# A streaming-encoder trunk on one Trainium2 core: pooled-channel forms tied to earlier products, and row-norm roots in two GpSimd operations

## The chip, the core and the metric

One core of one Trainium2 chip runs the whole kernel. The metric is the device time of one execution in microseconds. The engines are named as in the profile: PE (TensorE, matrix products), ACT (ScalarE), DVE (VectorE), POOL (GpSimd), SP (SyncE, which here issues DMAs). Each engine works through its own queue of instructions in order, and waits at its head for what an instruction needs.

## What is computed

A sequence of 2048 rows of 1024 channels goes through one layer with two branches and a feed-forward part:

```python
xn = rmsnorm(x, norm1_g[l])
z = xn @ w_in[l]
u_pool, zq, zf, zi, zo, zg = jnp.split(z, splits, axis=-1)
gates = jax.nn.sigmoid(zg + b_gate[l]).reshape(B, S, N_BRANCHES, D_MODEL)
ya = pool_mixer(u_pool, pool_w[l], pool_scale[l]) @ w_pa[l]
yb = hgrn2_mixer(zq, zf, zi, zo, lower_bounds[l], hgrn_norm_g[l]) @ w_pb[l]
merged = gates[:, :, 0] * ya + gates[:, :, 1] * yb
x = x + merged @ w_o[l]
x = x + conv_glu_ffn(rmsnorm(x, norm2_g[l]), w_up[l], conv_w[l], conv_b[l], w_down[l])
return rmsnorm(x, final_g)
```

`pool_mixer` takes trailing means over windows of 2, 4, 8 and 16 rows, less the row itself, through a small matrix per group of 128 channels: 512 pooled channels. `hgrn2_mixer` is a gated linear recurrence with four heads. The change touches how the operands of `... @ w_pa` are made ready, the roots inside `rmsnorm`, and the order of a few instructions in the last `rmsnorm`.

## The kernel before

**Halves and blocks.** The sequence is worked in two halves of 1024 rows (their tiles are named x0, mf0, gr0, pa0 ... and x2, mf2, gr2, pa2 ...; in the profile's short names the number is often left out). A half has two blocks of 512 rows, hf = 0 and 1. Each half runs first the mixer (input projection, recurrence, the two branch projections pa and pb, the output projection wo) and then the feed-forward part (up, dn). Activations lie with channels on the 128 partitions and 512 rows along the free axis, so almost every tile is 128 x 512.

**Products by seven.** A projection of two blocks by two groups of channels is one *unit*: a 2 x 2 product of blocks in Strassen's manner, seven products P1 to P7 in place of eight, in the order P1, P6, P5, P7, P2, P4, P3 (`ORDER`). Each product needs one *form* of the activations, a block or a sum or difference of blocks: P1 takes B11, P2 B21, P3 B22, P4 T4, P5 T1, P6 T2, P7 T3. A unit has three banks of PSUM: X for P1 and P2, Z for P6, P7 and P4, V for P5 and P3. Between products DVE reads a bank into a temporary: u2 after P6 (L1202), u3 after P7 (L1206). The next product on Z is written over what they have read: P7 waits for u2, P4 for u3.

**Precision.** Every operand is split in two fp32r parts, high and low, and a product takes three matmuls (high x high, high x low, low x high). `split` makes the parts of a form: the high part by a cast on ACT (L659), the low part by a subtraction on DVE (L660), and the subtraction needs the cast. Weights come by DMA into `raw` tiles, some are summed there by POOL (L446), and are split in the same way by L231 (ACT) and L232 (DVE) into `ops` tiles, six of which are alive.

**What runs around the change.** After the last unit of the input projection (a gate unit, gr0_7 in half 0) comes the pa projection of the pooled channels. It runs in two rounds d = 0, 1 of two units each, seven products per unit. A product of pa's first unit has k = 2 pieces, six matmuls, and the second unit's product follows it with the same form. The forms of pa, B11 to B22, two tiles each (j = 0, 1: names like mf0T40 and mf0T41, with h or l behind them for the part), are made by `pa_task`: it loads the eight tiles of pooled channels (`mx`) that were stored to DRAM earlier, takes differences (`minus`, L1479 on DVE, t3 on POOL) and splits them. Meanwhile the fourth head of the recurrence ends: its small matmuls (po, pv) stand between PE's large ones, its norm root on POOL (L693, L694), its gated output ot on DVE (L1141), and its transposes pt on PE.

**What sets the order.** The kernel is written as one main line of matmuls and a set of tasks, generators that are advanced by one step every six matmuls (`tick`). `yield n` puts a task's next step n ticks later. `place[0]` counts products from the last gate unit's P1 on: 1 to 7 there, then 8 for pa's P1, 9 P6, 10 P5, 11 P7, 12 P2, 13 P4, 14 P3. `pa_task` starts at the gate unit's P1 and waits before each form until `place[0]` has come to a number. A form's instructions get a dependency on the matmul last written (`in_turn`), which only the scheduler sees: the scheduler, which fills the engines' queues ahead of the run by its own timeline, doesn't put them ahead of it. `behind` is a dependency of the same kind between two named instructions. So the numbers in `pa_task` move instructions within the queues of ACT, DVE and POOL, and once the queues are fixed nothing overtakes.

**Row norms.** `row_rstd` (L697) takes 128 rows: two squares on ACT with their sums in two columns, then the root of mean square on POOL. `norm_rows` scales the rows by it (L719). The final norm of the last half is `final_last` (L1776): squares on ACT, root by `Sqrt` on ACT (L1785) and one refinement on DVE, then one half of the rows' channels scaled on ACT (`scale`, L1796), the other on DVE (L1804); `scale` of one tile of rows is written down during the next tile's `final_last`.

## Time and profile before

| | before |
|---|---|
| median of 3 runs | 2529.55 us (2528.21 to 2531.17) |
| profiled execution | 2528.86 us, its span 2527.1 us |
| mean granted clock of PE | 0.996 |
| PE busy | 2503.3 us, 99% of the span, 11460 instructions |
| PE weight loads | 2049.4 us, 81% |
| DVE busy | 1992.4 us, 79% |
| ACT busy | 1215.1 us, 48% |
| POOL busy | 814.2 us, 32% |

The span runs from the first to the last instruction of the profiled execution; its time has 1.8 us around that. Engines run beside each other, so the busy shares don't add up. In the views, a line such as `PE pa_Z L148 <- ACT mf0T41h L659` reads: a matmul into bank Z of pa (line 148 of the code) waited for the cast of form T4, second tile, high part (line 659) on ACT. A timeline row has its start, its length, engine, line, operation, output <- inputs and shape, and in brackets the idle time of that engine before it with what ended it. Rows of matmuls overlap, since they are pipelined; the step from start to start is what one costs.

### The profile page before, as it was taken

What the parts mean: (1) busy time and instruction counts of PE and PEld (TensorE: products, weight loads), DVE (VectorE), ACT (ScalarE), POOL (GpSimd) and SP (SyncE); (2) the same over time, 40 slices, a digit from 0 to 9 for tenths busy, and PEclk for the clock granted to TensorE, in tenths of its full rate; (3) what the DMA queues carried; (4) which work ended last, traced back from release to release, by engine and by line L of the source; (5) the groups of instructions that cost most, each with busy time, mean ns of one, the idle gap of its engine ahead of it and who ended that gap; (6) DMA issues with size and microseconds to landing.
All of it is one profiled execution on the core that took longest, in us unless ns stands there. A gap on an engine that the chain in (4) does not pass through costs nothing.

```text
span 2527.1 us, 35765 instructions
## 1 busy us (share of the span) xinstructions
PE 2503.3 (99%) x11460; PEld 2049.4 (81%) x11460; DVE 1992.4 (79%) x3528; ACT 1215.1 (48%) x2286; POOL 814.2 (32%) x1171
## 2 busy tenths in 40 slices
PE   9999999999999999999999999999999999999998
PEld 7888888788888888888888888887888888888886
DVE  7788878797998778875596778778979888778755
ACT  6534443434555544553554434543355555445534
POOL 4343453403354333541320202123033432325410
PEclk9999999999999999999999999999999999999999
DMA  8877787677898789897344343446343454447852
GB/s 272 272 199 225 209 222 232 203 226 244 204 257 238 228 225 243 270 358 237 113 155 153 106 133 109 144 157 229 125 157 119 151 153 135 151 133 245 321 166 97
DMA packets 252332, 493.76 MB, mean 195 GB/s; under 512 B 26544, under 2 KB 43056, under 8 KB 251824
## 3 DMA queue, kind: packets, MB, share of 16 engines
q1 hardware_dynamic: 184512, 313.60, 38.2%
q0 software_dynamic: 42656, 112.74, 17.4%
q10 hardware_dynamic: 24976, 65.13, 7.5%
q8 instruction: 91, 1.49, 0.2%
q14 instruction: 97, 0.79, 0.1%
HBM read 381.79 MB, written 187.17 MB: 225 GB/s over the span
## 4 chain that ended last, share of the span: by engine, by line
PE 97%; DVE 1%; ACT 1%; DMA 0%; issue 0%; POOL 0%; SPq 0%; DVEq 0%; POOLq 0%; ACTq 0%
PE dn_P L148 16%; PE up_Z L148 15%; PE up_V L148 10%; PE up_X L148 10%; PE wo_P L148 6%; PE gr_Z L148 5%; PE gr_V L148 4%; PE pb L148 4%; PE gr_X L148 4%; PE io_Z L148 3%; PE fr_Z L148 3%; PE io_V L148 2%; PE fr_V L148 2%; PE fr_X L148 2%; PE pl L1029 2%; PE pa_Z L148 1%
## 5 line engine op out<-in xcount | busy, mean ns | idle before, releaser
L231 ACT CAST ops<-raw 128x512 fp32r<-128x512 f32 x794 | 490.2, 620 | 867.4 <-PE dn_P L148 178.8
L232 DVE TENSOR_TENSOR ops<-raw,ops 128x512 fp32r<-128x512 f32 x794 | 588.1, 744 | 217.4 <-ACT ops L231 210.6
L1707 DVE SCALAR_TENSOR_TENSOR e<-h,cols,e 128x512 f32<-128x512 f32 x176 | 142.4, 813 | 30.4 <-ACT e L1705 23.9
L1705 ACT ACTIVATE e<-h,cols 128x512 f32<-128x512 f32 x176 | 142.2, 814 | 25.2 <-DVE h L1162 18.4
L1710 DVE SCALAR_TENSOR_TENSOR e<-h,cols,e 128x512 f32<-128x512 f32 x176 | 134.9, 776 | 2.5
L964 POOL DMA_DIRECT2D g_P<-dg_P x154 | 83.8, 545 | 161.7 <-PE dn_P L148 113.8
L1275 POOL TENSOR_TENSOR gf_P<-e,e 128x512 f32<-128x512 f32 x44 | 61.6, 1403 | 150.3 <-DVE e L1716 96.1
L446 POOL TENSOR_TENSOR raw<-raw,raw 128x512 f32<-128x512 f32 x36 | 51.1, 1420 | 154.7 <-DVE ops L232 138.7
L1275 POOL TENSOR_TENSOR gf_P<-gf_P,e 128x512 f32<-128x512 f32 x44 | 59.1, 1344 | 72.1 <-DVE e L1716 71.6
L1700 POOL COPY h<-h 128x2 f32<-128x2 f32 x88 | 40.0, 466 | 117.1 <-DVE h L1161 107.5
L1415 POOL TENSOR_TENSOR q<-q,qs 128x512 f32<-128x512 f32 x16 | 21.8, 1363 | 168.0 <-ACT qs L1414 165.6
L1714 ACT ACTIVATE e<-e 128x512 f32<-128x512 f32 x88 | 55.6, 632 | 37.1 <-DVE e L1710 37.0
L1702 POOL COPY hist<-h 128x2 f32<-128x2 f32 x88 | 35.1, 399 | 115.8 <-DVE h L1162 114.0
L1162 DVE TENSOR_TENSOR h<-up_u,up_V 128x512 f32<-128x512 f32 x88 | 60.1, 683 | 10.5 <-PE up_V L148 10.1
L1452 ACT ACTIVATE gt<-gt,cols 128x512 f32<-128x512 f32 x48 | 34.8, 725 | 66.8 <-DVE gt L1162 56.5
L1250 DVE TENSOR_TENSOR x<-x,wo_P 128x512 f32<-128x512 f32 x88 | 56.0, 682 | 12.0 <-PE wo_P L148 11.8
L1250 DVE TENSOR_TENSOR ac<-ac,dn_P 128x512 f32<-128x512 f32 x72 | 47.1, 682 | 17.5 <-PE dn_P L148 17.3
L1014 POOL COPY qm<-q 128x64 f32<-128x64 f32 x64 | 27.1, 446 | 99.6 <-DVE q L1046 19.6
L1700 POOL COPY h<-hist 128x2 f32<-128x2 f32 x88 | 45.2, 521 | 27.3 <-DVE m_T42l L660 27.2
L1200 ACT COPY up_e<-up_X 128x512 f32<-128x512 f32 x44 | 25.8, 586 | 57.7 <-PE up_X L148 50.5
L1730 POOL DMA_DIRECT2D dg_P<-gf_P x88 | 50.7, 576 | 8.1 <-POOL gf_P L1275 7.4
L1590 POOL TENSOR_TENSOR ya<-ya,gl 128x512 f32<-128x512 f32 x24 | 36.7, 1533 | 45.8 <-DVE ya L1587 20.8
(1372 smaller groups left out, 8130.6 us busy)
## 6 DMA issues: line engine op xcount, KB each, us to landing
g_P<-dg_P POOLq DMA_DIRECT2D x154, 256.0 KB, 6.0
raw<-in_w_up_t SPq DMA_DIRECT2D x132, 256.0 KB, 3.1
raw<-in_w_in_t SPq DMA_DIRECT2D x98, 256.0 KB, 3.2
dg_P<-gf_P POOLq DMA_DIRECT2D x88, 256.0 KB, 3.8
dg_P<-e SPq DMA_DIRECT2D x66, 256.0 KB, 3.6
raw<-in_w_dn SPq DMA_DIRECT2D x66, 256.0 KB, 4.1
x<-in_x SPq DMA_DIRECT2D x64, 256.0 KB, 5.2
gd<-gt ACTq DMA_DIRECT2D x64, 256.0 KB, 3.0
```

The costliest lines, as they stand in the source:

```text
L148: count[1] = pe.matmul(*args, **kw)
L231: self.mark = act.copy(hi, v)
L232: low = self.low = dve.tensor_tensor(lo, v, f32(hi), ALU.subtract)
L964: eng.dma_start(t, d)
L1162: return dve.tensor_tensor(dst, t, ps, ALU.add if how == "add" else ALU.subtract)
L1250: dve.tensor_tensor(t, t, ps[j], ALU.add if sg > 0 else ALU.subtract)
L1275: pin(eng.tensor_tensor(t, x0, x1, op))
L1700: pool.tensor_copy(h[:, 0:2], hist[:, mt] if hf == 0 else hs[s, 0][:, TB : TB + 2])
L1705: in_turn(act.activation(t, h[:, 2:], AF.Identity, bias=col(o_cb + mt), scale=col(o_cw + 4 * MF + mt)))
L1707: in_turn(second(dve.scalar_tensor_tensor(t, h[:, 1 : 1 + TB], col(o_cw + 2 * MF + mt), t, ALU.mult, ALU.add)))
L1710: dve.scalar_tensor_tensor(t, h[:, 0:TB], col(o_cw + mt), t, ALU.mult, ALU.add)
L1714: in_turn(act.activation(g, g, AF.Silu))
```

## The change

Three edits. In `pa_task` the numbers of `place[0]` go down: for B11 from 3 to 2, T2 4 to 3, T3's difference and T1 6 to 5, T3 8 to 6, B21 9 to 7, T4 10 to 8, B22 11 to 10, and the pauses of two ticks become one. In `row_rstd` the sum of the two squares and the constant is one POOL operation (a `tensor_scalar` with the first sum as its operand) where it was two, the first of them ahead of the second square. In `final_last` the scaling of the tile before is placed behind this tile's square root in the plan.

```diff
--- before.py
+++ after.py
@@ -699,10 +699,8 @@
         for hf in range(2):
             act.activation(junk[hf], halves[hf], AF.Square, scale=1.0 / 32.0,
                            accum_out=ss[:, hf : hf + 1])
-            if not hf:
-                pool.tensor_scalar(ss[:, 2:3], ss[:, 0:1], EPS, None, ALU.add)
         r = small.tile([P, 4], F32, tag="rstd", name=name + "r")
-        pool.tensor_tensor(r[:, 1:2], ss[:, 1:2], ss[:, 2:3], ALU.add)
+        pool.tensor_scalar(r[:, 1:2], ss[:, 1:2], ss[:, 0:1], EPS, ALU.add, ALU.add)
         last_root[0] = pool.tensor_tensor(r[:, :1], r[:, 1:2], neghalf[:, :1], ALU.pow)
         return r
 
@@ -1479,48 +1477,48 @@
                 in_turn(eng.tensor_tensor(x, x0, x1, ALU.subtract))
                 return x
 
-            while place[0] < 3:
+            while place[0] < 2:
                 yield 1
             for j in range(2):
                 form("B11", j, t[0, j])
                 yield 1
             t1, t2 = [], []
-            while place[0] < 4:
+            while place[0] < 3:
                 yield 1
             for j in range(2):
                 t1.append(minus("t1", j, t[1, j], t[0, j]))
                 t2.append(minus("t2", j, t[1, j + 2], t1[j]))
                 form("T2", j, t2[j])
-                yield 2
-            while place[0] < 6:
+                yield 1
+            while place[0] < 5:
                 yield 1
             t3 = [minus("t3", j, t[1, j], t[1, j + 2], pool) for j in range(2)]
             for j in range(2):
                 form("T1", j, t1[j])
                 yield 1
-            while place[0] < 8:
+            while place[0] < 6:
                 yield 1
             for j in range(2):
                 form("T3", j, t3[j])
-                yield 2
-            while place[0] < 9:
+                yield 1
+            while place[0] < 7:
                 yield 1
             for j in range(2):
                 form("B21", j, t[0, j + 2])
-                yield 2
-            while place[0] < 10:
+                yield 1
+            while place[0] < 8:
                 yield 1
             for j in range(2):
                 t4 = minus("t4", j, t[0, j + 2], t2[j])
                 form("T4", j, t4)
-                yield 2
-            while place[0] < 11:
+                yield 1
+            while place[0] < 10:
                 yield 1
             for j in range(2):
                 x = slot(f"mf{b0}_b22{j}")
                 in_turn(act.activation(x, t[1, j + 2], AF.Copy, scale=-1.0))
                 form("B22", j, x)
-                yield 2
+                yield 1
 
         emits = {"fq": emit_fq, "u": emit_u, "g": emit_g}
         oT = {}
@@ -1782,7 +1780,7 @@
             if not hf:
                 dve.tensor_scalar(ss[:, 2:3], ss[:, 0:1], EPS, None, ALU.add)
             r = small.tile([P, 4], F32, tag="rstd", name=f"f{b0}_{hf}_{j}r")
-            act.activation(r[:, 0:1], ss[:, 1:2], AF.Sqrt, bias=ss[:, 2:3])
+            root = act.activation(r[:, 0:1], ss[:, 1:2], AF.Sqrt, bias=ss[:, 2:3])
             dve.tensor_tensor(ss[:, 3:4], ss[:, 1:2], ss[:, 2:3], ALU.add)
             dve.reciprocal(r[:, 1:2], r[:, 0:1])
             dve.scalar_tensor_tensor(r[:, 2:3], r[:, 1:2], ss[:, 3:4], r[:, 1:2],
@@ -1792,12 +1790,14 @@
             rr = (b0 + hf) * TB + j * P
             o = [out[rr : rr + P, 512 * c : 512 * c + 512] for c in range(2)]
 
-            def scale():
-                act.activation(res[0], halves[0], AF.Copy, scale=r[:, 0:1])
+            def scale(other=None):
+                ins = act.activation(res[0], halves[0], AF.Copy, scale=r[:, 0:1])
+                if other is not None:
+                    behind(ins, other)
                 act.dma_start(o[0], res[0])
 
             while scales:
-                scales.pop()()
+                scales.pop()(root)
             if hf:
                 scales.append(scale)
             for c in range(hf, 2):
```

The order of instructions moves in the last part of the mixer, from the last gate unit's P5 to the wo projection, in both halves in the same way; elsewhere the roots lose one row each (32 rows of L703), and ACT's last rows change. Line numbers in the changed kernel are two lower from L705 to the middle of `final_last` (L1479 is L1477 there, L1206 is L1204).

DVE's queue around u3 of the last gate unit in half 0 (`ss`, `st` are the recurrence's state, `gt` a gate). Before:

```order
L660 TENSOR_TENSOR mf0B111l_4698<-mx0_1_4623,mf0B111h_4697 128x512
L1120 SCALAR_TENSOR_TENSOR st3_1_129<-ss0_3_4672,f0_3_3983,pv0_3_4667 128x128
L1206 TENSOR_TENSOR gr0_7_u3_4701<-gr0_7_Z_4609,gr0_7_e1_4607 128x512
L1162 TENSOR_TENSOR gt1_1_7_4703<-gr0_7_u3_4701,gr0_7_V_4645 128x512
L1479 TENSOR_TENSOR mf0_t10_4721<-mx1_0_4625,mx0_0_4621 128x512
L1479 TENSOR_TENSOR mf0_t20_4723<-mx1_2_4627,mf0_t10_4721 128x512
```

The same place now:

```order
L660 TENSOR_TENSOR mf0B111l_4674<-mx0_1_4615,mf0B111h_4673 128x512
L1477 TENSOR_TENSOR mf0_t10_4687<-mx1_0_4617,mx0_0_4613 128x512
L1118 SCALAR_TENSOR_TENSOR ss0_3_4668<-ss0_3_4668,f0_3_3975,pv0_3_4663 128x128
L1477 TENSOR_TENSOR mf0_t20_4689<-mx1_2_4619,mf0_t10_4687 128x512
L1118 SCALAR_TENSOR_TENSOR st3_1_129<-ss0_3_4668,f0_3_3975,pv0_3_4663 128x128
L660 TENSOR_TENSOR mf0T20l_4692<-mf0_t20_4689,mf0T20h_4691 128x512
L1477 TENSOR_TENSOR mf0_t11_4701<-mx1_1_4621,mx0_1_4615 128x512
L1477 TENSOR_TENSOR mf0_t21_4703<-mx1_3_4623,mf0_t11_4701 128x512
L660 TENSOR_TENSOR mf0T21l_4706<-mf0_t21_4703,mf0T21h_4705 128x512
L1204 TENSOR_TENSOR gr0_7_u3_4709<-gr0_7_Z_4601,gr0_7_e1_4599 128x512
L1160 TENSOR_TENSOR gt1_1_7_4711<-gr0_7_u3_4709,gr0_7_V_4637 128x512
```

The differences t10, t20, t11, t21 and both low parts of T2 now stand ahead of u3. On PE three rows of the fourth head (po1_3) now stand ahead of this unit's P4, and on POOL the differences t30, t31 ahead of the norm root ro0_3.

DVE's queue around the u2 of pa's second unit, first round, half 0. Before:

```order
L660 TENSOR_TENSOR mf0T31l_4898<-mf0_t31_4812,mf0T31h_4897 128x512
L1202 TENSOR_TENSOR pa0_0_u2_4901<-pa0_0_e1_4870,pa0_0_Z_4885 128x512
L1141 SCALAR_TENSOR_TENSOR ot1_3_4919<-po1_3_4829,ro1_3_4844,z1_3_4753 128x128 x4
L1202 TENSOR_TENSOR pa0_1_u2_4924<-pa0_1_e1_4879,pa0_1_Z_4903 128x512
L232 TENSOR_TENSOR ops134_4964<-raw97_4560,ops134_4964 128x512
L660 TENSOR_TENSOR mf0B210l_4944<-mx0_2_4633,mf0B210h_4943 128x512
L660 TENSOR_TENSOR mf0B211l_4968<-mx0_3_4635,mf0B211h_4967 128x512
```

The same place now:

```order
L660 TENSOR_TENSOR mf0B211l_4880<-mx0_3_4627,mf0B211h_4879 128x512
L1477 TENSOR_TENSOR mf0_t40_4901<-mx0_2_4625,mf0_t20_4689 128x512
L232 TENSOR_TENSOR ops134_4984<-raw97_4552,ops134_4984 128x512
L660 TENSOR_TENSOR mf0T40l_4904<-mf0_t40_4901,mf0T40h_4903 128x512
L1200 TENSOR_TENSOR pa0_0_u2_4907<-pa0_0_e1_4870,pa0_0_Z_4889 128x512
L1139 SCALAR_TENSOR_TENSOR ot1_3_4925<-po1_3_4829,ro1_3_4844,z1_3_4753 128x128 x4
L1477 TENSOR_TENSOR mf0_t41_4930<-mx0_3_4627,mf0_t21_4703 128x512
L660 TENSOR_TENSOR mf0T41l_4933<-mf0_t41_4930,mf0T41h_4932 128x512
L1200 TENSOR_TENSOR pa0_1_u2_4936<-pa0_1_e1_4883,pa0_1_Z_4909 128x512
L660 TENSOR_TENSOR mf0B220l_4958<-mf0_b220_4955,mf0B220h_4957 128x512
L660 TENSOR_TENSOR mf0B221l_4971<-mf0_b221_4968,mf0B221h_4970 128x512
```

The second unit's u2 now has both tiles of T4 and of B21 ahead of it, and the low parts of B22 stand right behind it. Before, T4's first difference came eight rows behind this u2.

ACT's queue in the last rows of the kernel, for the third tile of rows and the fourth (the number before the last in f2_1_2r and f2_1_3r counts them). Before:

```order
L1766 ACTIVATE fj2_1_3_1_24574,fss2_1_3_23933<-ac2_1_3_1_22752 128x512
L1796 ACTIVATE fo2_1_2_0_24548<-ac2_1_2_0_23350,f2_1_2r_24550 128x512
L1785 ACTIVATE f2_1_3r_24578<-fss2_1_3_23933 128x1
L1797 DMA out_0<-fo2_1_2_0_24548 128x512
L1796 ACTIVATE fo2_1_3_0_24576<-ac2_1_3_0_23352,f2_1_3r_24578 128x512
```

Now:

```order
L1764 ACTIVATE fj2_1_3_1_24542,fss2_1_3_23901<-ac2_1_3_1_22718 128x512
L1783 ACTIVATE f2_1_3r_24546<-fss2_1_3_23901 128x1
L1794 ACTIVATE fo2_1_2_0_24516<-ac2_1_2_0_23318,f2_1_2r_24518 128x512
L1797 DMA out_0<-fo2_1_2_0_24516 128x512
L1794 ACTIVATE fo2_1_3_0_24544<-ac2_1_3_0_23320,f2_1_3r_24546 128x512
```

The square root of the last tile now stands ahead of the scaling of the tile before it.

## The prediction

> **What bounds the kernel now.** I read the chain of waits first. It ends on TensorE:
>
> ```profile
> PE 97%; DVE 1%; ACT 1%; DMA 0%; issue 0%; POOL 0%; SPq 0%; DVEq 0%; POOLq 0%; ACTq 0%
> ```
>
> So only time in which PE stands, or runs at a lower clock, can be won. The waits of PE (summed us, count, longest) say where it stands:
>
> ```profile
> PE x_t L725 <- DVE x_xs L719: 2.5, 4, 1.0
> PE pa_Z L148 <- ACT mf0T41h L659: 1.7, 1, 1.7
> PE pa_Z L148 <- ACT mf2T41h L659: 1.7, 1, 1.7
> PE pa_Z L148 <- DVE mf0T41l L660: 1.3, 1, 1.3
> PE pa_V L148 <- ACT mf0B221h L659: 0.6, 1, 0.6
> ```
>
> Nearly all of them name forms T4 and B22 of the pooled channels, once in each half (mf0, mf2). The windows around them (us, PE busy, granted clock, DMA) give the price:
>
> ```profile
> 444.31:459.13 14.82, 14.82 (x71) 1.00 0.73 248
> 459.13:464.70 5.57, 1.90 (x5) 0.98 0.01 2
> 464.70:474.60 9.90, 8.19 (x18) 0.50 0.80 265
> 1712.49:1717.00 4.51, 1.41 (x5) 1.00 0.00 0
> 1717.00:1724.40 7.40, 5.68 (x12) 0.54 0.73 252
> ```
>
> PE stands for most of 5.57 us, and afterwards works for 9.9 us at half the clock; the second half shows the same with 7.4 us. PE's timeline (start, us) gives the ends of the stretch:
>
> ```profile
> 456.34 0.40 PE L148 MATMUL pa_X<-mf0B210h,ops 128*128 128x512 f32 x1
> 458.90 0.40 PE L148 MATMUL pa_X<-mf0B211h,ops 128*128 128x512 f32 x1
> 460.14 0.49 PE L148 MATMUL pa_Z<-mf0T40h,ops 128*128 128x512 f32 x1 [0.84 <-ACT mf0T40h L659]
> 461.51 0.40 PE L148 MATMUL pa_Z<-mf0T40h,ops 128*128 128x512 f32 x1
> 463.62 0.50 PE L148 MATMUL pa_Z<-mf0T41h,ops 128*128 128x512 f32 x1 [1.71 <-ACT mf0T41h L659]
> 466.40 0.63 PE L148 MATMUL pa_Z<-mf0T40h,ops 128*128 128x512 f32 x1
> 468.53 0.63 PE L148 MATMUL pa_Z<-mf0T41h,ops 128*128 128x512 f32 x1
> 475.36 0.40 PE L148 MATMUL pa_X<-mf0B110h,ops 128*128 128x512 f32 x1
> ```
>
> ```profile
> 1712.26 0.40 PE L148 MATMUL pa_X<-mf2B211h,ops 128*128 128x512 f32 x1
> 1727.61 0.40 PE L148 MATMUL pa_X<-mf2B110h,ops 128*128 128x512 f32 x1
> ```
>
> The twelve matmuls of P2 from 456.34 to 458.90 step by 2.56 / 11 = 0.232 us. The 24 of P4 and P3 behind them should take 5.6. In half 0 they run from 459.13 (458.90 + 0.23) to 475.36: 16.23, a loss of **10.6**. In half 1 from 1712.49 to 1727.61: 15.12, a loss of **9.5**. Together 20.1 us; no other stretch costs PE as much. The slow clock's part: from 466.40 to 468.53 five matmuls step by 0.426, so the 18 in half 0's slow window lost 18 × 0.194 = 3.5 and the 12 in half 1's 2.3; the rest is standing.
>
> The last forms are late because DVE and ACT reach them only when PE already wants them. Thresholds lower by one or two products cure that, if what is pushed aside has slack.
>
> **The change, part by part.**
>
> *Forms earlier: what is won.* T4's and B22's operations stand some ten DVE rows earlier. By the walk below the last T4 low ends at 458.1 and the last B22 low at 460.0, while PE comes to P4 at about 463 and to P3 at 465.7. Both waits and the slow clock behind them go: the whole 20.1 us. The loads are no bar. The pooled channels come by eight transfers:
>
> ```profile
> 420.71 4.93 SPq L964 DMA_DIRECT2D mx<-md  x8
> DMA to landing us min/median/max: 4.5/5.8/6.3
> ```
>
> The third, which the first difference needs at 431.7, is issued by 420.71 + 3/8 of 4.93 = 422.6 and there by 428.9; the last by 431.9, long before B21.
>
> *What is pushed aside.* DVE and POOL take turns where both read two operands from SBUF:
>
> ```profile
> 429.37 1.27 POOL L446 TENSOR_TENSOR w128s<-raw,raw 128x512 f32<-128x512 f32 x1
> 429.66 1.53 DVE L660 TENSOR_TENSOR mf0B110l<-mx,mf0B110h 128x512 fp32r<-128x512 f32 x1
> 431.37 0.68 DVE L660 TENSOR_TENSOR mf0B111l<-mx,mf0B111h 128x512 fp32r<-128x512 f32 x1
> 432.92 0.69 DVE L1206 TENSOR_TENSOR gr_u<-gr_Z,gr_e 128x512 f32<-128x512 f32 x1 [0.61 <-PE gr_Z L148]
> 436.97 0.48 PE L148 MATMUL gr_Z<-x_T40h,ops 128*128 128x512 f32 x1
> ```
>
> Alone, such a DVE operation is 0.68 long and the next starts 0.60 later (431.37 to 431.98 in the queue). The one at 429.66 ran beside POOL's sum and took 1.53: it ended 0.55 after POOL did. So I price 0.60 each, and a POOL sum in the way holds DVE until it ends, up to 1.27 us. The Trainium skill, page "SBUF — State Buffer", section "Who interferes with whom", says the same in its words: a DVE instruction with two SBUF inputs contends with a GpSimd one that reads SBUF, and the first one keeps the shared ports for its whole length. The rows above agree (1.53 against 0.68). That rule speaks against this change, which brings the forms' differences closer to POOL's sums.
>
> *Wait A, the last gate unit's P4.* It overwrites the bank that u3 (L1206) reads. u3 was at 432.92 after a free 0.61; now t20, T20l, t11, t21 and T21l and the first difference t10 stand ahead of it: six operations, 3.6 us. Without any hold u3 ends at 432.92 − 0.61 + 3.6 + 0.60 = 436.5. PE comes to P4 at 436.97 + 0.67 = 437.64, since three instructions of po1_3 (0.22 each, an estimate from the steps of the same multiplications around 436) now stand ahead: no wait. At most three POOL operations meet those six (the third sum and the two differences t3 that POOL now makes in front of its norm root): 3 × 1.27 = 3.8, so u3 ends at 440.3, a wait of 2.7. Walking the queues by their rows: B110l ends 428.65, B111l 430.45, POOL's third sum runs 430.45 to 431.7 and holds t10 to 432.3; POOL's t30 (432.25 to 433.5) holds t20 to 434.1; t31 (434.05 to 435.3) holds T20l to 435.9; then t11 436.5, t21 437.3, T21l 438.6 behind its ACT cast, u3 439.3. **A = 1.65 us**, bounds 0 and 2.7. I take the walk, near the upper end, because the collisions that it counts are of the kind seen at 429.66.
>
> *Wait B, the second pa unit's P7.* It overwrites the bank that its u2 reads:
>
> ```profile
> 451.38 0.68 DVE L1202 TENSOR_TENSOR pa_u<-pa_e,pa_Z 128x512 f32<-128x512 f32 x1
> 451.98 0.68 DVE L232 TENSOR_TENSOR ops<-raw,ops 128x512 fp32r<-128x512 f32 x1
> 454.88 0.48 PE L148 MATMUL pa_Z<-mf0T30h,ops 128*128 128x512 f32 x1
> ```
>
> u2 ended at 451.98; PE wanted the bank at 454.88, or now, 1.65 later, at about 456.6. Ahead of u2 now stand weight 134, B210l, B211l, t40, T40l, t41 and T41l as well: 7 × 0.60 = 4.2, so 456.2 without any hold and no wait. With A's delay in full (1.65 + 0.67) and one POOL sum (1.27) it is 459.8: 3.2. The walk: T31l and B210l, B211l end 451.25, t40 451.85, weight 134 453.0, T40l 453.6, the first unit's u2 454.3, ot1_3 455.25, t41 held by POOL's sum until 456.1 and done 456.7, its cast on ACT 457.45, T41l 458.1, u2 458.8. PE waits from 456.6: **B = 2.15 us**, bounds 0 and 3.2, and again I take the walk. Behind it 6 + 12 matmuls lead to P4 at 458.8 + 18 × 0.232 = 463.0, past T41l's 458.1.
>
> Does the clock fall at A or B? In half 0 PE stood through most of 459.13 to 461.51 (two matmuls in the 2.4 us, 1.9 of them idle), and the window to 464.70 still shows 0.98; it fell only after the further gap before 463.62 (2.11 from 461.51, less a step of 0.23: 1.88). Two lone waits of 1.65 and 2.15 with 17 us of work between them should not do it. The Trainium skill, page "TensorE: Matmul & The Clock Gate", section "What's actually happening", has the clock halved after an idle window of about 3.4 us. The trace fits that: the fall stands at the end of 459.13 to 464.70, where PE is busy 1.90 of 5.57. By it neither wait alone would halve the clock.
>
> *The roots of row norms* lose one of three POOL instructions in 32 places. PE waits for a norm only at the start (the row of x_t above), and there the last tile's scaling stands in DVE's queue behind a weight's low part, not behind the root:
>
> ```profile
> 10.58 0.52 POOL L703 TENSOR_SCALAR x_3ss<-x_3ss 128x1 f32<-128x1 f32 x1
> 11.18 0.28 POOL L705 TENSOR_TENSOR x_3r<-x_3ss 128x1 f32<-128x1 f32 x1
> 11.54 0.57 POOL L706 TENSOR_TENSOR x_3r<-x_3r,neghalf 128x1 f32<-128x1 f32 x1
> 11.71 0.69 DVE L232 TENSOR_TENSOR ops<-raw,ops 128x512 fp32r<-128x512 f32 x1 [0.30 <-ACT ops L231]
> 12.32 0.88 DVE L719 TENSOR_SCALAR x_xs<-x,x_3r 128x512 f32<-128x512 f32 x2
> ```
>
> L703 ran beside the row's second square and the root was done at 12.11, with DVE busy until 12.32: nothing to win. The new first operation is a tensor_scalar; if it takes L703's 0.52 where L705 took 0.28, the root comes at 12.35, 0.03 late. If the weight's part did not cover it, the same 0.24 would be lost. So 0, with bounds 0 and +0.24.
>
> *The tail.* The last square root waited on ACT behind the scaling of the tile before:
>
> ```profile
> 2520.20 0.19 ACT L1766 ACTIVATION_READ_ACCUMULATOR fj<-ac 128x1 f32 x1
> 2520.29 0.70 ACT L1796 ACTIVATE fo<-ac,f_2r 128x512 f32<-128x512 f32 x1
> 2520.90 0.28 ACT L1785 ACTIVATE f_3r<-fss 128x1 f32<-128x1 f32 x1
> 2522.05 0.75 DVE L1804 SCALAR_TENSOR_TENSOR fo<-ac,f_3r,fg 128x512 f32<-128x512 f32 x1
> ```
>
> It can start near 2520.35, right behind the sum of squares: **0.55 us** off a chain that nothing else covers. The scaling that it overtakes ends by 2521.3, ahead of the last one at 2522.05. Bounds 0.3 and 0.6.
>
> **The sum.** Per half A + B = 3.8 us in place of 10.6 and 9.5: 6.8 + 5.7 = 12.5. With the tail 13.05. The profiled execution took 2528.86 (span 2527.1, the rest lies around it), so 2515.8; it stands 0.7 under the median of the runs, 2529.55, which becomes **2516.5**.
>
> **The rivals.**
>
> *No wait at A and B* (the lower bounds): 20.1 + 0.55 = 20.65 less, 2508.9. For it: the collisions with POOL may fall otherwise, and t3 itself waits for free slots, which the walk gives it early. Against: the DVE rows alone use up nearly all the slack (436.5 against 437.64, and 456.2 against 456.6). Chance 0.13.
>
> *The clock falls at one of the new waits.* A fall costs what it cost now, 3.5 or 2.3. In one half or in both: 2516.5 + 2.3 to 2516.5 + 5.8, so 2518.8 to 2522.3. For it: 2.15 us is a longer single gap than the 1.88 that preceded the fall. Against: there it came on top of the two shorter gaps before 461.51. Chance 0.15.
>
> *The wait is only moved.* The slower end: u3 at A and u2 at B come at their upper bounds (2.7 + 3.2 = 5.9 per half) and each wait halves the clock for 9.9 us, now full of work (9.9 × 0.194 / 0.426 = 4.5 each): 14.9 per half, 29.8 against 20.1 + 0.55, so 9.1 us **slower**, 2538.7. It is one mechanism, DVE's queue of forms in front of the reads that free Z; it decides from a loss of 10.3 us per half on. For it: DVE's order here is fixed by the plan, u3 and u2 can't overtake. Against: it needs every POOL hold in full. Chance 0.05; what lies between (2524.5 to 2534.6, say A and B at their bounds with one fall in each half) has 0.07. That the places don't change the order can be left out: the order of DVE's queue does differ.
>
> **How the numbers follow.** The forecast with both waits near their walked sizes, 2513 to 2519, has 0.60. The range for 8 in 10 takes in the second case nearly whole and the first down to its bound: 2509 to 2523. 0.2% is about 5 us, what a measurement of this kernel can tell from no change: under 2524.5 is faster, 0.60 + 0.13 + 0.15 = 0.88; within it 0.07; slower 0.05.
>
> **What would show it.** Right: no wait of PE on T41 or B221, the clock at 1.00 from 444 to 480 and in the same place of the second half, one wait of 1 to 2.5 us before gr_Z's P4 and one before pa_Z's second P7, both released by DVE, and the tail's square root 0.6 earlier. Wrong: those two waits absent (then 2509), a granted clock near 0.5 right behind one of them (2519 and more), or PE waiting for a weight (ops) that DVE now splits later than the forms; that last would show that the DVE queue, not the forms, sets this stretch.

## The result, and the profile after

| | before | after |
|---|---|---|
| median | 2529.91 us (4 runs, 2528.21 to 2531.17) | 2513.73 us (4 runs, 2512.86 to 2516.28) |
| ratio | | 0.9938, interval 0.9921 to 0.9955 |
| profiled execution, its span | 2528.86, 2527.1 us | 2514.4, 2512.7 us |
| granted clock | 0.996 | 0.998 |

The kernel is 16.2 us faster by the medians and 14.4 us by the spans of the two profiled executions (a span runs from the first to the last instruction). The waits of PE in the changed kernel (us in total, times, longest):

```profile
PE pa_Z L148 <- DVE pa_u L1200: 4.1, 2, 2.1
PE x_t L723 <- DVE x_xs L717: 2.7, 2, 2.1
PE gr_Z L148 <- DVE gr_u L1204: 1.9, 2, 1.0
PE warm L685 <- POOL ident L566: 1.4, 1, 1.4
PE io_Z L148 <- ACT ops L231: 0.6, 1, 0.6
```

No line names T4 or B22 any more. Their place is taken by two waits for DVE's reads of a bank: u3 of the last gate unit (wait A) and u2 of pa's second unit (wait B), each once in either half, as the order of DVE's queue had it. PE's timeline in half 0 has them:

```profile
437.70 0.39 PE L1126 MATMUL po<-v,at 128*128 128x128 f32 x2
439.04 0.50 PE L148 MATMUL gr_Z<-x_T40h,ops 128*128 128x512 f32 x1 [0.95 <-DVE gr_u L1204]
458.64 0.50 PE L148 MATMUL pa_Z<-mf0T30h,ops 128*128 128x512 f32 x1 [2.07 <-DVE pa_u L1200]
463.62 0.40 PE L148 MATMUL pa_Z<-mf0T41h,ops 128*128 128x512 f32 x1
468.48 0.39 PE L148 MATMUL pa_X<-mf0B110h,ops 128*128 128x512 f32 x1
```

T41, for which PE stood 1.71 us before, comes now with no bracket: nothing waits. The second round's first product starts at 468.48 where it started at 475.36. DVE's and POOL's rows behind A and B:

```profile
430.46 1.79 DVE L1477 TENSOR_TENSOR mf_t<-mx,mx 128x512 f32<-128x512 f32 x1
432.43 1.53 DVE L1477 TENSOR_TENSOR mf_t<-mx,mf_t 128x512 f32<-128x512 f32 x1
434.64 1.03 DVE L660 TENSOR_TENSOR mf0T20l<-mf_t,mf0T20h 128x512 fp32r<-128x512 f32 x1 [0.43 <-ACT mf0T20h L659]
438.30 0.68 DVE L1204 TENSOR_TENSOR gr_u<-gr_Z,gr_e 128x512 f32<-128x512 f32 x1
457.91 0.68 DVE L1200 TENSOR_TENSOR pa_u<-pa_e,pa_Z 128x512 f32<-128x512 f32 x1
```

```profile
429.92 1.78 POOL L446 TENSOR_TENSOR w128s<-raw,raw 128x512 f32<-128x512 f32 x1
431.66 3.47 POOL L1477 TENSOR_TENSOR mf_t<-mx,mx 128x512 f32<-128x512 f32 x2
```

t10, t20 and T20l (1.79, 1.53 and 1.03 in place of 0.68) end right behind POOL's sum and its two differences t3: 431.70, 433.41 and 435.13 on POOL, 432.25, 433.96 and 435.67 on DVE, 0.55 later each time.

What one would not see from the waits is the clock. The windows of PE (us, PE busy, granted clock, DMA) around B in half 0 (two rows) and half 1 (three):

```profile
454.94:458.35 3.41, 1.63 (x10) 1.00 0.94 315
458.35:461.76 3.41, 3.12 (x13) 1.00 0.43 161
1700.80:1704.22 3.42, 1.39 (x9) 1.00 0.84 288
1704.22:1707.63 3.41, 3.41 (x10) 0.50 0.28 104
1707.63:1711.04 3.41, 3.41 (x16) 1.00 0.00 0
```

In half 1 the same wait of 2 us was followed by 3.41 us at half the clock (a *slow window* from here on). It cost 7 matmuls 0.2 us each, about 1.5 us. The four runs of the changed kernel differ in the same sense: spans of 2511.1 and 2511.3 at a mean granted clock of 0.999 and 1.000, 2512.7 (the profiled one) at 0.998 and 2514.6 at 0.997. The profiled one had a second slow window at the start, from 7.80 to 11.21, behind 3.42 us in which PE was busy 1.30; its first matmul of the input projection (14.26) came no later than in e2 below (14.25), where the clock there was full.

**Where the 14.45 us of span came from**, from PE's start times at the same matmuls in both traces. "Stretch" is the time from the last gr_Z matmul of P7 to the first P1 matmul of pa's second round, less 32.3 us: 121 large matmuls (that gr_Z one counted) at 0.232 and the 38 small ones at 0.111 (40 or 42 in e9 to e11, counted so). What is left is what PE lost there, its *loss*.

| | before | after | gain |
|---|---|---|---|
| start, to the first matmul of the input projection | 13.97 | 14.26 | −0.3 |
| loss of the stretch, half 0 | 10.6 | 3.5 | 7.1 |
| loss of the stretch, half 1 | 9.5 | 5.1 | 4.4 |
| norm of half 1, first x_t to first io_X | 14.02 | 13.11 | 0.9 |
| last dn_P matmul to the end | 8.64 | 7.85 | 0.8 |
| all other parts, none over 0.7 | | | 1.5 |

The largest of the other parts, 0.6, are the up products of half 1 (426.1 before, 425.5 now), which the change doesn't touch; the last section comes back to it.

### The profile page after: what moved, and what is told of

Its sections match the earlier page's. It is cut to its first block, busy times and chain, and to the rows that moved or that the text cites. A ratio compares the mean times of both kernels' runs of the same rounds, so it can differ in the third digit from the quotient of the medians.

```text
span 2512.7 us, 35696 instructions
## 1 busy us (share of the span) xinstructions
PE 2494.6 (99%) x11460; PEld 2048.8 (82%) x11460; DVE 1996.1 (79%) x3528; ACT 1214.1 (48%) x2286; POOL 808.3 (32%) x1139
## 4 chain that ended last, share of the span: by engine, by line
PE 98%; DVE 1%; ACT 1%; DMA 0%; issue 0%; POOL 0%; SPq 0%; ACTq 0%
PE dn_P L148 17%; PE up_Z L148 15%; PE up_X L148 10%; PE up_V L148 10%; PE wo_P L148 6%; PE gr_Z L148 5%; PE gr_V L148 4%; PE pb L148 4%; PE gr_X L148 3%; PE io_Z L148 3%; PE fr_Z L148 3%; PE fr_V L148 2%; PE fr_X L148 2%; PE io_V L148 2%; PE pl L1027 2%; PE ur_Z L148 1%
## 5 line engine op out<-in xcount | busy, mean ns | idle before, releaser
L232 DVE TENSOR_TENSOR ops<-raw,ops 128x512 fp32r<-128x512 f32 x794 | 596.4, 755 | 206.2 <-ACT ops L231 199.4
L1027 PE MATMUL pl<-qm,k 128*128 128x192 f32 x256 | 50.2, 326 | 0.0
```

The costliest lines, as they stand in the source:

```text
L232: low = self.low = dve.tensor_tensor(lo, v, f32(hi), ALU.subtract)
L1027: ins = pe.matmul(pa_[:, c * 192 : c * 192 + 192], ks[:, (i + c) * P : (i + c + 1) * P], mv[:, c].rearrange("p s x -> p (s x)"), start=Tru ...
```

## The experiments

Each batch of runs had its own runs of the kernel before, with medians of 2528.41 to 2530.37 us; the ratios are against these. e0, e2, e3 and e8 ran once each and have no interval. Spans are of single profiled executions.

**The kernel before, once more (e0), and each edit alone (e1, e2, e3).**

```diff
 e1: pa_task of the change; row_rstd and final_last of before
 e2: row_rstd of the change; the rest of before
 e3: final_last of the change; the rest of before
```

> The kernel before once more, unchanged, for how far two profiled executions of one program stand apart, in the places read here: the first matmul of the input projection, the stretch between the two mixers, and the end. Theory: the 0.4 us that the changed kernel gained between 548 and 1264 and the 0.7 after 1840 are such differences, so this one shows a few tenths there too. Rival: it repeats the first profile to 0.1 us, and the changed kernel gained there.

> Only the new numbers in pa_task; roots and tail as before. Theory (the forms are the whole gain but for the tail): the span is shorter than that of the kernel before by 14.5 less the tail's 0.5 to 0.9, so by 13.6 to 14, and PE's waits are gr_Z for u3 (about 1.0, twice) and pa_Z for u2 (about 2.1, twice) as in the changed kernel. Rival (the roots bring part of it, by a shorter norm): under 12.5 us.

> Only the roots in two POOL operations. Theory: no gain; the first matmul of the input projection starts 0.3 us later than in the kernel before (14.26 in the changed kernel against 13.97), because the new operation is longer and ends later; the rest within 0.5. Rival (the missing POOL operation saves about 0.2 us per norm at places where PE waits): 0.5 us or more shorter, first matmul at 13.9 or earlier.

> Only the order of the last rows on ACT. Theory: the distance from the last dn_P matmul to the end of the span is 0.5 to 0.6 us shorter than in the kernel before, nothing else moves. Rival (0.85, as the difference of the two traces has it between the last dn_P matmul and the end): 0.8 to 0.9. Second rival (the landing of the last transfer varies by more): outside both.

Spans: e0 2528.3, e1 2516.7 (median 2517.52, ratio 0.9950, interval 0.9934 to 0.9967), e2 2526.1, e3 2527.5, against 2527.1 and, for the change, 2512.7.

e0: the same program ran 1.1 us longer than in the first profile. The start was 0.3 later, the stretch of half 0 lost 10.8 and not 10.6, the norm of half 1 took 14.22; the other parts agreed to 0.1 but for the way to half 0's stretch (0.4). So a term of a few tenths can't be read off two single profiles. The stretch is also that of the kernel before in e2 and e3: there it lost 9.4 and 10.9 in half 0 and 9.4 twice in half 1, so the gain of 7.1 in half 0 is known to about 1 us. The expectation named the stretch between 548 and 1264 for such scatter; apart from the norm it was not there.

e1: 10.4 us less than before by the span, not 13.6 to 14, and under the 12.5 at which the rival was to hold: it lacks 4.0 us of the whole change. 0.7 of them are the tail. 1.5 are in half 0's stretch (loss 5.0): wait B was the same to 0.01 us, but there the clock fell too. 1.7 are in the norm of half 1, 14.85 against 13.11; the first and e0's profile, with neither edit, had 14.02 and 14.22. There PE waited for a scaled tile, and POOL's roots, three operations each, run in a chain:

```profile
1256.53 0.66 PE L725 MATMUL x_t<-ident,x_xs 128*128 128x128 f32 x4 [0.80 <-DVE x_xs L719]
```

```profile
1254.42 0.52 POOL L703 TENSOR_SCALAR x_2ss<-x_2ss 128x1 f32<-128x1 f32 x1
1255.02 0.28 POOL L705 TENSOR_TENSOR x_2r<-x_2ss 128x1 f32<-128x1 f32 x1
1255.38 0.57 POOL L706 TENSOR_TENSOR x_2r<-x_2r,neghalf 128x1 f32<-128x1 f32 x1
1256.04 0.51 POOL L703 TENSOR_SCALAR x_3ss<-x_3ss 128x1 f32<-128x1 f32 x1
```

One root there takes 1.62 (1254.42 to 1256.04). In the changed kernel the roots start 1.38 and 1.60 apart by turns:

```profile
1250.72 0.59 POOL L703 TENSOR_SCALAR x_1r<-x_1ss 128x1 f32<-128x1 f32 x1
1252.10 0.87 POOL L703 TENSOR_SCALAR x_2r<-x_2ss 128x1 f32<-128x1 f32 x1
1253.70 0.59 POOL L703 TENSOR_SCALAR x_3r<-x_3ss 128x1 f32<-128x1 f32 x1
1254.38 0.60 POOL L704 TENSOR_TENSOR x_3r<-x_3r,neghalf 128x1 f32<-128x1 f32 x1
```

From the end of the last square to the end of the last scaling it is 7.94 us in e1 (1250.88 to 1258.82) and 6.40 in the changed kernel (1249.56 to 1255.96). But e2, with the new roots alone, did not win it: its norm took 14.06, with one PE wait of 0.7. Its span is 1.0 shorter than the first profile's, but its stretch of half 0, which the roots don't touch, lost 1.1 less; so neither the 0.5 of its rival nor the theory's "no gain" can be read from the span. Over all profiles this part takes 14.0 to 14.9 with the old roots (four) and 13.1 to 13.3 in seven of the nine that have them beside the new places, and 14.0 and 14.1 in the other two (e8, e10). So the two edits together bring something like 0.9 us at this norm, where the places alone cost it 0.6 to 0.8; what the roots do by themselves isn't shown. The start was 0.28 later in e2 than in the first profile (14.25), but e0's was 0.30 later with the old roots: the loss of 0.3 at the start is scatter too, within what these runs can tell.

e3: the last dn_P matmul to the end took 8.25, 0.39 less than before, outside both the theory and the first rival; e2, which doesn't touch the tail, had 8.28. The rows up to the last scalings are the steadier measure. In the changed kernel:

```profile
2504.84 0.40 PE L148 MATMUL dn_P<-ops,dn_P_10l 128*128 128x512 f32 x1
2506.53 0.19 ACT L1764 ACTIVATION_READ_ACCUMULATOR fj<-ac 128x1 f32 x1
2506.75 0.29 ACT L1783 ACTIVATE f_3r<-fss 128x1 f32<-128x1 f32 x1
2507.91 0.75 DVE L1804 SCALAR_TENSOR_TENSOR fo<-ac,f_3r,fg 128x512 f32<-128x512 f32 x1
2508.07 0.72 ACT L1794 ACTIVATE fo<-ac,f_3r 128x512 f32<-128x512 f32 x1 [0.42 <-DVE f_3r L1789]
```

From the last dn_P matmul to the end of the span (2512.69) it is 7.85. From the read-out of the sum to DVE's scaling it is 1.38 us, where both scalings started 1.85 behind it before (2520.20 to 2522.05). ACT's now starts last, 1.54 behind the read-out (1.55 in e3), because ACT first does the scaling that the root overtook (to 2507.65) and issues its transfer (0.34). So the order on ACT brings 0.47 on DVE's half and 0.31 on ACT's, which ends last. The rest up to 0.8 lies behind it, in the last transfers and what follows them. The 0.8 repeats: the changed kernel and e4 to e11 take 7.8 to 7.9 from the last dn_P matmul, the kernel before, e0 and e1 8.6 to 8.7. Why e2 and e3 lie between isn't settled.

**Is wait A a price of its own (e4)?** T2's number back at 4, so that u3 stands ahead of T2's rows again.

```diff
-            while place[0] < 3:
+            while place[0] < 4:
                 yield 1
             for j in range(2):
                 t1.append(minus("t1", j, t[1, j], t[0, j]))
```

> The changed kernel with T2's number back at 4: in DVE's queue u3 of the last gate unit stands ahead of the differences and of T2's low parts again, all later forms stay early. Theory (DVE's forms ahead of u3 make the wait at gr_Z): that wait is gone, and the wait of pa_Z for u2 stays at 1 to 2.1, so 1 to 2 us shorter than the changed kernel over both halves. Rival (the delay only moves on to u2, which ends when it did): the wait for u2 grows by the 1.0 that PE comes earlier, to about 3, and the total is the same as the changed kernel's within 0.4.

Median 2519.54, ratio 0.9959 (0.9945 to 0.9972); the span is 4.7 us longer than the changed kernel's. Wait A is gone, and PE's one remaining group of waits has grown:

```profile
PE pa_Z L148 <- DVE pa_u L1200: 8.0, 4, 2.3
```

```profile
440.97 1.79 DVE L660 TENSOR_TENSOR mf0T21l<-mf_t,mf0T21h 128x512 fp32r<-128x512 f32 x1
442.68 1.78 DVE L660 TENSOR_TENSOR mf0T10l<-mf_t,mf0T10h 128x512 fp32r<-128x512 f32 x1
444.38 1.78 DVE L660 TENSOR_TENSOR mf0T11l<-mf_t,mf0T11h 128x512 fp32r<-128x512 f32 x1
458.33 0.68 DVE L1200 TENSOR_TENSOR pa_u<-pa_e,pa_Z 128x512 f32<-128x512 f32 x1
```

DVE reads the second u2 at 458.33, where the changed kernel had it at 457.91. What it saved ahead of u3 it lost by low parts that POOL now held at another place (three of 1.78), so PE, which came earlier, stood longer: 1.71 at the first unit's u2 and 2.28 at the second's. Half 0 got a slow window on top. The two stretches lost 1.8 us more than the changed kernel's; another 1.7 lie in the up products of half 1, where PE never waits (the last section). The theory that A could be won by order alone fell. The rival's mechanism holds, the delay moved on to u2; its sizes don't: it had one wait of about 3 and the same total within 0.4.

**Is wait B (e5)?** T4's number back at 10; u2 of both units stands ahead of T4.

```diff
-            while place[0] < 8:
+            while place[0] < 10:
                 yield 1
             for j in range(2):
                 t4 = minus("t4", j, t[0, j + 2], t2[j])
```

> The changed kernel with T4's number back at 10: DVE reads u2 of both pa units ahead of T4's forms; T2 stays ahead of u3. Theory: the wait for u2 (2.1 per half) is gone, the one for u3 (1.0) stays, and T4 and B22 are still in time, so 4.1 us shorter than the changed kernel. Rival (T4 two products later is late again): PE waits for T41 or B221 by 1 us or more and the gain is under 2, or a loss if the clock falls again.

Median 2513.18, ratio 0.9934 (0.9919 to 0.9949), the same as the changed kernel within what these runs can tell. B is gone and no window of the stretch was slow; P4 waits 0.3 and 1.0 for u3 of pa, which now stands behind T4. The stretches lost 1.6 and 2.7 us, 4.3 less than in the changed kernel, near the 4.1 expected. But of that 0.9 and 1.0 came back behind them, between the second round's start and wo (64.65 against 63.8 and 63.7), where the second round's P7 now waits 0.4 for its u2 in either half, and 0.8 in the up products of half 0, so that the span is 1.1 shorter and the time the same.

**Both (e6).** T2 at 4 and T4 at 10.

> T2 at 4 and T4 at 10, the rest as in the changed kernel. Theory: neither wait is left, 3.1 us per half, 6.2 us shorter than the changed kernel: span near 2506.5. Rival (what is won at u3 is lost again at T4 or B22): PE waits for T41h, T41l or B221 and the span stays above 2509.

Median 2517.38, ratio 0.9949 (0.9936 to 0.9961), a span 3.0 us longer than the changed kernel's, where 6.2 shorter was expected. The two stretches together lost 8.1 us, against 8.6: nothing won. The rest of the 3.0 lies outside, 1.2 of it in the up products of half 0 and 0.9 between the second round and wo in half 1. It was not T41 or B221 that PE waited for, as the rival had it, but the third of DVE's reads:

```profile
PE pa_Z L148 <- DVE pa_u L1204: 5.7, 3, 3.3
```

```profile
455.78 1.83 DVE L660 TENSOR_TENSOR mf0T40l<-mf_t,mf0T40h 128x512 fp32r<-128x512 f32 x1
457.53 1.77 DVE L1477 TENSOR_TENSOR mf_t<-mx,mf_t 128x512 f32<-128x512 f32 x1
461.78 0.68 DVE L1204 TENSOR_TENSOR pa_u<-pa_Z,pa_e 128x512 f32<-128x512 f32 x1
```

With A and B both out of the way, T4's rows stand in front of pa's u3 and are held there by POOL's sums (and twice, for 0.68 and 0.49, DVE waits for ACT's casts). DVE's reads of u3, u2 and u3 and the forms are one queue. Its order decides where PE waits; the work and the holds in it decide how long.

**Do POOL's differences hold DVE (e7)?** T3's differences and T1 at 6, T3 at 7.

```diff
-            while place[0] < 5:
+            while place[0] < 6:
                 yield 1
             t3 = [minus("t3", j, t[1, j], t[1, j + 2], pool) for j in range(2)]
```

> The changed kernel with the number for T3's differences and T1 at 6 in place of 5 and T3's at 7: on POOL the two differences t3 go behind the norm root, while DVE's rows up to u3 stay the same (T2 still ahead of it). T4 falls behind u2 by it. Theory (POOL's t3 operations hold DVE's t20 and T20l, about 1.2 us): the wait of gr_Z for u3 falls from 1.0 to under 0.2, and that for u2 is gone as well. Rival (six DVE operations ahead of u3 and the two ACT casts make the delay, POOL doesn't matter): 0.8 to 1.0 stays at gr_Z.

Yes. DVE's rows up to u3 are the same, POOL does t3 later, and the rows that were 1.53 and 1.03 are 0.68 and 0.69; u3 comes 1.19 earlier, and PE doesn't wait for it. DVE, POOL and PE in half 0 of e7:

```profile
432.43 0.68 DVE L1477 TENSOR_TENSOR mf_t<-mx,mf_t 128x512 f32<-128x512 f32 x1
433.79 0.69 DVE L660 TENSOR_TENSOR mf0T20l<-mf_t,mf0T20h 128x512 fp32r<-128x512 f32 x1 [0.43 <-ACT mf0T20h L659]
437.11 0.68 DVE L1204 TENSOR_TENSOR gr_u<-gr_Z,gr_e 128x512 f32<-128x512 f32 x1
```

```profile
439.55 3.01 POOL L1477 TENSOR_TENSOR mf_t<-mx,mx 128x512 f32<-128x512 f32 x2
```

```profile
437.85 0.50 PE L148 MATMUL gr_Z<-x_T40h,ops 128*128 128x512 f32 x1
```

The stretch lost 2.2 us in either half, 1.6 of it now in front of P4; 0.6 and 1.6 came back between the second round and wo, and the median, 2514.46 (ratio 0.9938, 0.9924 to 0.9951), is the changed kernel's.

**Three more DVE rows in front of u2 (e8).** T4's second difference is taken four times.

```diff
                 t4 = minus("t4", j, t[0, j + 2], t2[j])
+                for _ in range(3 * j):
+                    in_turn(dve.tensor_tensor(t4, t[0, j + 2], t2[j], ALU.subtract))
```

> The changed kernel with T4's second difference taken four times instead of once, the same operation on the same tiles, so three more DVE rows of 0.6 ahead of the second unit's u2. Theory 1 (DVE's rows ahead of u2 set the wait, and the clock halves for 3.41 us after every window of 3.41 us in which PE worked under 0.4 of the time; so read from the runs so far): the wait grows by 1.8 to about 4.0 in both halves, 3.6 in all, and with such a wait a window under 0.4 is near certain, so both halves have a slow window of about 1.5 us of loss where the changed kernel had one: 5.1 longer than the changed kernel. Theory 2 (the clock only falls after a window that PE stood through, 3.41 us whole; a wait of 4.0 covers one only by chance): 3.6 longer, or less, as one slow window goes too.

The span is 2521.0, 8.3 us longer than the changed kernel's. Wait B grew from 2.1 to 4.2 us (8.5 in total for both halves), so three rows of 0.6 and a little more. Both halves had a slow window, as theory 1 had it, and lost 7.3 and 7.1 us in the stretch, 5.8 more than the change (5.1 was expected); the other 2.5 lie elsewhere, 0.9 of them in the norm of half 1. As a separate test of the two theories on the clock this run is weak: in half 1 PE stood through one window whole, in half 0 nearly.

```profile
458.23:461.64 3.41, 0.57 (x2) 1.00 0.34 115
461.64:465.05 3.41, 3.41 (x10) 0.50 0.20 77
1707.50:1710.91 3.41, 0.00 (x0) 1.00 0.55 187
```

**Less work in the stretch (e9, e10, e11).** pa_task starts during the last gate unit but one, so that B11 and T2 are made while DVE is idle; T4 is at 10.

```diff
+                if n == len(PROJ) - 2 and p == "P7":
+                    mtask = Task(pa_task())
                 if n == len(PROJ) - 1:
                     if p == "P1":
                         quiet[0] = True
-                        mtask = Task(pa_task())
...
-            while place[0] < 2:
+            while place[0] < 1:
...
-            while place[0] < 3:
+            while place[0] < 1:
...
-            while place[0] < 8:
+            while place[0] < 10:
```

> pa_task starts at P7 of the last gate unit but one, so that the pooled channels come five transfers earlier on SP and the forms B11 and T2 are made where DVE stood idle (2.9 us ahead of 426 and 2.2 ahead of 422); T4's number is 10 as in e5. Theory (DVE's whole work between 426 and P4 is the bound of this stretch, and each order only moves the wait): five to eight rows fewer behind 426, 3 to 4.8 us; the loss of 3.5 and 5.1 per half in the changed kernel falls to under 1, so 6 to 8 us shorter, a span of 2505 to 2507. Rival (not the work but its order was the bound, and e5 has the best order): as e5, 2511 to 2512. Second rival (the loads push weights back): PE waits for ops, 2513 or more.

> As e9, but pa_task starts two products later, at P4 of the last gate unit but one: in SP's queue the loads then stand behind the transfer that stores a weight's sum (kwg7ins2), which in e9 stood behind seven loads and held ACT and then DVE for 5.2 us in half 0. Theory (in e9 that late store took back what the earlier forms won in half 0): half 0 loses about 0.9 as e9's half 1 did, where it lost 3.3, so 2.4 us shorter than e9, a span near 2508.6. Rival (half 0's DVE stood for another reason, the weight itself): half 0 loses 3 again.

> e10 with T3's differences and T1 at 6 and T3 at 7 as in e7, so that POOL's t3 go behind the norm root. Theory (POOL's operations hold DVE in front of u3): no wait at gr_Z in either half and up to 1 us per half less than e10. Rival (what is won there is lost at P4, which waits for u3 of pa behind T4 and B22): within 0.5 of e10.

e10 has P4 where e9 has P7 in the first line; e11 is e10 with T1 at 6 and T3 at 7. Medians 2512.78 (ratio 0.9937, 0.9923 to 0.9950), 2513.45 (0.9936, 0.9922 to 0.9950) and 2515.44 (0.9946, 0.9933 to 0.9958): none beats the change. In half 1 of e9 and of e10 the stretch lost only 0.9 us, as the theory had it for both halves. In half 0 e9 lost 3.3, because DVE stood for ACT, and ACT for a store that the new loads had got in front of:

```profile
426.49 0.69 DVE L232 TENSOR_TENSOR ops<-raw,ops 128x512 fp32r<-128x512 f32 x1 [5.18 <-ACT ops L231]
```

```profile
422.99 0.69 ACT L1450 ACTIVATE gt<-gr_X,cols 128x512 f32<-128x512 f32 x1 [3.42 <-DMA kwg7ins<-w121s]
```

e10 mended that and lost 2.1 there, not 0.9; then the loads themselves were late for B11. In both, 0.7 to 0.9 us per half of what the stretch won was lost again behind it, up to wo. e11's rival held in its mechanism: no wait A, but waits of 2.3 and 1.6 us in front of P4. It came out 2 us longer than e10, not within 0.5, and is the slowest of the three.

| loss of the stretch, us | half 0 | half 1 | slow windows in it |
|---|---|---|---|
| the change | 3.5 | 5.1 | half 1 |
| e1 places alone | 5.0 | 5.1 | both |
| e4 u3 first | 6.0 | 4.4 | half 0 |
| e5 u2 first | 1.6 | 2.7 | none |
| e6 both first | 5.2 | 2.9 | half 0 |
| e7 t3 late | 2.2 | 2.2 | none |
| e8 more rows | 7.3 | 7.1 | both |
| e9 early loads | 3.3 | 0.9 | none |
| e10 early loads, later | 2.1 | 0.9 | none |
| e11 early loads, t3 late | 3.1 | 2.1 | none |

## Why the prediction was right, and where its steps were off

*The forms come in time.* Right, and the main term: the losses of 10.6 and 9.5 us that it was to take away are gone, no matmul waits for T4 or B22, and the slow clock behind them went too.

*Waits A and B.* Their places and releasers were right. B was 2.1 in both halves for 2.15 predicted, A 1.0 for 1.65. The term of A was mis-sized by 0.6: u3 ended at 438.98 where the walk had 439.3, and PE came 0.3 later than the walk had it, at about 437.92 (437.70 and two small steps of 0.11). The holds by POOL, on which the walk and its choice near the upper bound rested, are shown by e7.

*"Two lone waits of 1.65 and 2.15 … should not do it."* This step failed in half 1. The clock fell behind B there, and it took 1.5 us; in e1, with the same waits, it fell in both halves. The step asked how long a gap is, and compared it with the sum of gaps before. What comes closest to deciding it is the share of work in a window on a fixed grid (the last section). The page "TensorE: Matmul & The Clock Gate" of the Trainium skill, section "What's actually happening", on which the prediction leaned beside the rows, has such a free-running window, but lets the clock fall after an idle one. If idle means without work, no such fall should have come; PE worked 1.39 of 3.41 us in the window before it. The trace of the kernel before, which the prediction took to fit, doesn't fit that either: on the grid the window ahead of its fall at 464.52 had 1.24 us of work:

```profile
461.11:464.52 3.41, 1.24 (x3) 1.00 0.00 0
```

The rival "the clock falls at one of the new waits" came true with its sign, a clock near 0.5 right behind B, but not its time: it priced a fall at 2.3 or 3.5; a single slow window costs 1.5.

*The two stretches together* gave 11.5 us for 12.5 predicted: A brought 1.2 more over both halves, the clock took 1.5, and the remaining 0.7 is in the ends of the waits (a restart steps by 0.34 and not 0.23) and in small gaps that the walk leaves out.

*"PE waits for a norm only at the start."* Right for the waits view, whose four waits of 2.5 us all lie there, but the norm of half 1 got 0.9 shorter. PE's gaps there were 0.27 and less over a step, too short for that row. Roots priced at 0 were mis-sized by up to 0.9; whether they do it alone is open.

*The tail.* 0.55 predicted. DVE's half gained 0.47, but ACT's half, which ends last, 0.31: the overtaken scaling did end ahead of it (2507.65), but the issue of its transfer on ACT (to 2508.02), which the prediction left out, holds ACT's last scaling to 2508.07. With the last transfers it is 0.8.

The total came out near for partly other reasons: 1.0 less from the stretches, 0.9 more from the norm, 0.25 from the tail, and 1.5 more spread over parts that the change doesn't touch, less 0.3 at the start. What made that 1.5 isn't settled. The spans of two profiles of one program (e0) lay 1.1 apart, but the 0.6 in the up products of half 1 is no scatter of that kind: there the first profile, e0 and e3 agree within 0.04.

*A and B as two prices.* The sum added them. It was near as a sum, but e4 shows that A could not have been taken off by itself, and e6 that both could not by order; e5 took B away and lost most of the gain elsewhere.

## What to carry to other kernels

Where one engine's queue both makes operands and reads out the banks that the bound engine will write next, moving one ahead moves the wait to the other. Look for the work, and for what holds it, before the order. A transfer or a form that is pulled ahead is paid by whatever stood in that place of its queue: follow that one first. A short wait of the bound engine is priced with the clock that it may cost, not by its length alone.

## What the runs showed of the hardware

The TensorE clock changed only on a grid of 3.41 us, and nearly each change follows from the window before. From the windows quoted and their like in the other runs: after PE was busy 1.39 (the change, half 1), 1.41 and 1.38 (e1), 1.28 (e4), 1.05 (e6) and 0.57 us (e8) of 3.41, and after 1.30 and 1.47 at the start of the change and of e8, the next window ran at half the clock. After 1.63 (the change, half 0), 1.73 and 2.06 (e4) and 1.87 (e6) it stayed full. So the border lies near 1.6 us of busy time in 3.41, but it isn't sharp: it also fell after 1.59 (e0, 469.30 to 472.72) and once after 1.93 (e3), and stayed full after 1.58 (e7, 2502.38 to 2505.79). The busy time has modelled ends, so that it counts a lone matmul for longer than its step; whether that makes the exception in e3 is open. A wait of 2.1 us can fall on either side of the border by where it lies on the grid. A slow window costs about 1.5 us, so by an estimate from these figures a kernel can gain or lose that much per half by its place on the grid. Rows of e4, which has both cases, and of e3's exception:

```profile
456.94:460.35 3.41, 1.28 (x6) 1.00 0.78 296
460.35:463.76 3.41, 3.41 (x10) 0.50 0.21 78
1706.20:1709.62 3.42, 1.73 (x8) 1.00 0.70 270
458.79:462.21 3.42, 1.93 (x6) 1.00 0.08 29
```

One window at half the clock with 3.1 us of work or more in it was enough to bring it back in all of the changed kernels; in the kernel before, whose PE kept waiting, the slow stretch of half 0 lasted three windows (464.5 to 474.8).

PE's step itself is not quite constant. Over the up products of half 0, some 425 us with no wait of PE in them, the first up matmul to the first dn matmul took 425.7 in the kernel before (425.69, 425.70 in e0) and in the change, 425.2 in e9, 426.3 in e4 and 426.9 in e6; in half 1 it was 426.1 in the kernel before (426.1 in e0, 426.2 in e3), 425.5 in the change and 427.2 in e4. That is up to 0.4% with the same 1856 matmuls, as large as the effects sought in e4 to e11, and where one program was profiled twice (the kernel before and e0) it repeated to 0.02 us. The cause is open.

DVE and POOL held each other both ways. DVE's rows grew from 0.68 to 1.5 to 1.8, and POOL's two differences took 3.47 us among DVE's rows and 3.01 where less stood beside them (e7).
